# Modulation and gate steps emitted behind the linear attention, and ordered behind low parts of weights

## The chip, the cores and the metric

The kernel runs on one core of one Trainium2 chip. The metric is the device time of one execution in microseconds, the lower the better. Five engines work side by side, each through its own list of instructions, strictly in the order of that list: TensorE (PE, with its weight loads as PEld), VectorE (DVE), ScalarE (ACT), GpSimd (POOL) and SyncE (SP), which here only issues transfers.

## The reference

A trunk of two layers on 512 tokens of width 1024, in float32:

```python
for i in range(2):
    shift, scale, gate = split(silu(c) @ w_ada + b_ada, 3)
    h = rms_norm(x, ln_pre) * (1 + scale) + shift
    u = split_columns(h @ w_in)            # 3740 columns
    o_a = dilated_attention(...)           # group A
    o_b = nsa_attention(...)               # group B: compressed, selected, window
    o_c = rms_norm(gla_attention(...))     # group C: gated linear attention
    o_d = banded_attention(..., sinks)     # group D
    y = concat(o_j * silu(z_j)) @ w_out
    x = x + gate * rms_norm(y, ln_post)
```

`shift`, `scale` and `gate` of a layer come from the vector c alone: 1024 by 3072 weights a layer, used once.

## The kernel before

Products that need float32 accuracy are made of three: every weight block and every activation is split into a high part (`whi`, `HH`: a copy on ScalarE) and a low part (`wlo`, `HL`: a subtraction on VectorE, for weights in `split_w`, line 494), and high by high, high by low and low by high are added up on TensorE (`mm_T` line 541, `mm_TM` line 552). Weights of `w_in` come in pieces of 512 KB through four buffers `wraw`; their two parts have three buffers each.

A layer is one loop, `merge` (line 1274 on): the attention generators are run in the order C (linear attention), B, A, D, and between their steps the projections of `w_in` (`proj`) and the first part of the output product (`out1`) are emitted, in amounts by estimated costs. Emission sets priorities; the tile framework then sorts each engine's list by them and by readiness, and that list is fixed when the kernel is built. Attention steps are emitted with a lead in priority (the numbers HC, HB, HA, HD).

The steps that the change moves are those of `extras(l)` (line 375), a third generator, `bg` in `merge`. It holds what the coming layer's norm and this layer's residual need of `w_ada`:

- for layer 1, emitted during layer 0: 32 **modulation steps**, each a load `wmod` of 256 KB and one multiply and sum on VectorE (`mod`, line 306), with a tiny step on line 310 after every fourth;
- for each layer, two **gate columns** of eight **gate steps**: a load `wada` of 256 KB and one multiply and add on VectorE (`mac`, lines 364 and 366) into `aac`. After the eighth, `fin` loads two broadcast rows (`adab`, `adal`), sums `aac` over partitions on TensorE (`ada`, line 393), adds on VectorE (line 394) and multiplies on GpSimd (`gl`, line 396).

All these loads, `adab` and `adal` included, share one tile tag `ad` with **two buffers**, and `aac` has one. The loads are issued by SyncE, whose list also holds the loads of weights and those of the linear attention (`vs`, line 840).

How fast `extras` advances is set by the list TK of each layer, one number for C, B, A and D:

```python
def bg(cost):
    tick[0] += cost
    while tick[0] > pace:
        tick[0] -= pace
        next(BG[0], None)
for n_, (g, names, ratio, lead) in enumerate(steps):
    pace = LP[l]['TK'][min(n_, 3)]
```

`cost` is the estimated time of the projection step just emitted. `tick` is not reset between C, B, A and D.

Of the kernel before, what the change touches and what calls it, by code (L numbers as in the profile page):

```python
# [7 lines left out]
F32 = mybir.dt.float32  # L8
F32R = mybir.dt.float32r
AF = mybir.ActivationFunctionType  # L10
ALU = mybir.AluOpType
# [31 lines left out]
STP = 0  # L43

LP = [
    dict(HC=30, HB=[60, 200, 120], HA=60, HD=200, RC=0.9, RB=0.7, RA=1.4, RD=0.8, TK=[1.5, 1.5, 1.5, 1.5], CY=(1, 3, 3), PT=(4, 3),
         HO=(0, 2, 1, 3)),
    dict(HC=30, HB=[0, -60, 200], HA=100, HD=30, RC=0.9, RB=0.8, RA=0.8, RD=1.4, TK=[1.0, 6.0, 1.2, 0.7], CY=(0, 2, 2), PT=(1, 0),
         HO=(0, 3, 1, 2)),
]  # L50
WLO_MOD, WLO_POOL = 5, ()
# [183 lines left out]
def build(tc, A, out_d):  # L235
    nc = tc.nc
    PE, ACT, DVE, POOL, SP = nc.tensor, nc.scalar, nc.vector, nc.gpsimd, nc.sync
    with ExitStack() as ctx:
        def pool(name, bufs, **kw):
            return ctx.enter_context(tc.tile_pool(name=name, bufs=bufs, **kw))  # L240
# [8 lines left out]
        ad_p = pool('ad', B['ad'])  # L249
# [9 lines left out]
        def ps_t(tag, name):  # L259
            return ps.tile([128, 512], F32, tag=tag, name=name)  # L260
# [4 lines left out]
        def s_t(name, n, bufs=None):  # L265
            return sm_p.tile([128, n], F32, tag=name, name=name, **({'bufs': bufs} if bufs else {}))
# [16 lines left out]
        def load_mod(l, n, p, tag):  # L283

            wt = p.tile([128, 512], F32, tag=tag, name='wmod')
            SP.dma_start(out=wt, in_=A['w_mod'][l, n // 4, n // 2 % 2, n % 2])
            return wt
# [13 lines left out]
        def mod(l, n, wt, ss, gs):  # L301

            o, c = _P['bada'][0], n // 2
            h = n % 2
            init, dst = (tmp[:, c:c + 1], ss[:, c:c + 1]) if h else (pars[l][:, o + c:o + c + 1], tmp[:, c:c + 1])
            DVE.tensor_tensor_reduce(wt, wt, csr[:, 512 * h:512 * h + 512], 0.5, init, ALU.mult, ALU.add, dst)  # L306
            if n % 4 == 3:
                j = n // 4
                o = _P['lnpre'][0]
                DVE.scalar_tensor_tensor(gs[:, j:j + 1], ss[:, c:c + 1], 1.0, pars[l][:, o + j:o + j + 1], op0=ALU.add, op1=ALU.mult)  # L310
# [3 lines left out]
        def load_par(l):  # L314
            t = pp.tile([128, P_TOT], F32, tag='par', name='par')
            SP.dma_start(out=t, in_=A['par'][l])
            pars.append(t)

        WR = {}
        for ch in FIRST:  # L320
# [8 lines left out]
            elif ch in 'TQ':  # L329
                n = 'tm_c' if ch == 'T' else 't_cqk'  # L330
# [31 lines left out]
        def mac(acc, w, k, first):  # L362
            if first:
                DVE.tensor_scalar(acc, w, csil[:, k:k + 1], None, op0=ALU.mult)
            else:
                DVE.scalar_tensor_tensor(acc, w, csil[:, k:k + 1], acc, op0=ALU.mult, op1=ALU.add)

        def halves(t):
# [3 lines left out]
            DVE.tensor_tensor(out=lo, in0=t, in1=hi, op=ALU.subtract)  # L372
            return hi, lo

        def extras(l):

            units = []
            if l + 1 < DEPTH:
                load_par(l + 1)
                ss, gs = s_t('adass', 16, 2), s_t('adags', 8, 2)  # L380
                ada[l + 1] = (gs, ss)
                units = [(2, n) for n in range(32)]
            units += [(n, k) for n in range(2) for k in range(8)]
            gl[l] = []

            def fin(n, sb):
                acc = ps_t('s', 'ada')
                o = 512 * n
                br = ad_p.tile([128, 512], F32, tag='ad', name='adab')
                SP.dma_start(out=br, in_=A['rows'][l, 0, :, o:o + 512].to_broadcast([128, 512]))  # L390
                lr = ad_p.tile([128, 512], F32, tag='ad', name='adal')
                SP.dma_start(out=lr, in_=A['rows'][l, 1, :, o:o + 512].to_broadcast([128, 512]))
                PE.matmul(acc, ones.to_broadcast([128, 128]), sb, start=True, stop=True)
                DVE.tensor_tensor(out=br, in0=acc, in1=br, op=ALU.add)  # L394
                g = sz_p.tile([128, 512], F32, tag='sz', name='gl')
                POOL.tensor_tensor(out=g, in0=br, in1=lr, op=ALU.mult)
                gl[l].append(g)

            def load(n, k):
                if n == 2:  # L400
                    return load_mod(l + 1, k, ad_p, 'ad')
                wt = ad_p.tile([128, 512], F32, tag='ad', name='wada')
                SP.dma_start(out=wt, in_=A['w_gate'][l, n, k])
                return wt
            nxt = load(*units[0])
            prev = None
            for u, (n, k) in enumerate(units):
                yield
                wt = nxt
                if prev:  # L410
                    fin(*prev)
                    prev = None
                if n == 2:
                    mod(l + 1, k, wt, ss, gs)
                else:
                    if k == 0:
                        sb = ad_p.tile([128, 512], F32, tag='aac', name='aac', bufs=1)
                    mac(sb, wt, k, k == 0)
                    if k == 7:
                        prev = (n, sb)  # L420
                if u + 1 < len(units):
                    nxt = load(*units[u + 1])
            yield
            fin(*prev)
# [63 lines left out]
        def split_w(raw, n, eng=None):  # L488
            hi = w_p.tile([128, n], F32R, tag='whi', name='whi')
            lo = w_p.tile([128, n], F32R, tag='wlo', name='wlo')  # L490
            ACT.copy(hi, raw)  # L491
            nsplit[0] += 1
            eng = eng or (POOL if nsplit[0] % WLO_MOD in WLO_POOL else DVE)
            eng.tensor_tensor(out=lo, in0=raw, in1=hi, op=ALU.subtract)  # L494
            return hi, lo

        def load_piece(l, name, i, kk, ncol):
            if l == 0 and i == 0 and WR.get(name):
                raw = WR[name].pop()
            else:  # L500
                raw = raw_p.tile([128, kk * ncol], F32, tag='raw', name='wraw')
                o = W_OFF[name, i]
                SP.dma_start(out=raw, in_=A['w_in'][l, o:o + 128 * kk * ncol].rearrange('(p n) -> p n', p=128))
            hi, lo = split_w(raw, kk * ncol, DVE if l == 0 and name in ('tm_c', 't_cqk') else None)
            return [(hi[:, j * ncol:(j + 1) * ncol], lo[:, j * ncol:(j + 1) * ncol]) for j in range(kk)]
# [657 lines left out]
        def wo_piece(l, n):  # L1163
            k0, kk, c, nc_ = WO_PIECES[n]
            raw = raw_p.tile([128, kk * nc_], F32, tag='raw', name='wor')
            o = WO_OFF[n]
            SP.dma_start(out=raw, in_=A['w_out'][l, o:o + 128 * kk * nc_].rearrange('(p n) -> p n', p=128))
            if k0 == 6:
                res = []
                for j in range(kk):  # L1170
                    r = raw[:, nc_ * j:nc_ * (j + 1)]
                    hi, lo = qk_pair('wo2')
                    ACT.copy(hi, r)
                    DVE.tensor_tensor(out=lo, in0=r, in1=hi, op=ALU.subtract)
                    res.append((hi, lo))
                return res
            hi, lo = split_w(raw, kk * nc_)
            return [(hi[:, nc_ * j:nc_ * (j + 1)], lo[:, nc_ * j:nc_ * (j + 1)]) for j in range(kk)]
# [146 lines left out]
        for l in range(DEPTH):  # L1325
            for n in list(T):
                if l and n not in ('cvd', 'vc', 'dv', 'bg'):
                    del T[n]
            BG[0] = extras(l)
            pg = chain(proj(l, 1 if l else 2), out1(l))  # L1330
            PG[0] = pg
# [34 lines left out]
def make(arrays):  # L1366
    import concourse.bacc as bacc
    nc = bacc.Bacc("TRN2", target_bir_lowering=False, num_devices=1)
    A = {n: nc.dram_tensor('in_' + n, arrays[n].shape, F32, kind="ExternalInput").ap() for n in _INS}
    out = nc.dram_tensor('out_y', (S, D), F32, kind="ExternalOutput").ap()  # L1370
    with tile.TileContext(nc, schedule_with_timeline_sim=TLS) as tc:
        build(tc, A, out)
    return nc
# [8 lines left out]
```

## Time and profile before

| what | value |
|---|---|
| time, median of 3 runs | 697.35 us (696.06 to 697.5) |
| time of the profiled execution | 696.35 us |
| its span, first to last instruction | 694.6 us |
| mean granted clock of TensorE | 0.984 |
| busy: PE, DVE, ACT, POOL | 93%, 71%, 49%, 4% of the span |
| transfers | 87.89 MB, mean 127 GB/s |

The span is what the trace covers; 1.75 us of the profiled execution lie around it. Busy time of PE is modelled, so what counts in it is rather where it is idle. The stages in this trace: start-up with the first projections to 48 us, layer 0's linear attention to 152 us, its other attention to about 300 us, output product and the turn to layer 1 to 384 us, layer 1's linear attention to 494 us, its other attention to about 630 us, and the last output product.

### The profile page before, as it was taken

How to read it: one execution, taken by the hardware profiler on the slowest of the kernel's cores; microseconds unless marked ns; L12 is line 12 of the kernel's file. 1: busy time of each engine (PE TensorE's matmuls, PEld its weight loads, DVE VectorE, ACT ScalarE, POOL GpSimd, SP SyncE). 2: the span in 40 equal slices, each digit the busy share in tenths (PEclk: the TensorE clock that was granted, in tenths of full speed). 3: DMA queues.
4: the chain of work that ended last, by engine and by line, in shares of the span. 5: the costliest groups of instructions: out<-in, count | busy, mean ns of one | idle time of the engine just before them, and what ended most of it. 6: DMA issues, size and time to landing. Idle time of an engine off the chain costs nothing.

```text
span 694.6 us, 11875 instructions
## 1 busy us (share of the span) xinstructions
PE 649.3 (93%) x4460; PEld 525.3 (76%) x4460; DVE 492.8 (71%) x1255; ACT 340.3 (49%) x744; POOL 29.5 (4%) x57
## 2 busy tenths in 40 slices
PE   3899789999999999999998989899999999999996
PEld 1787666877777677779897768678877877778895
DVE  2984888667976878774698457742699858768656
ACT  7554344164664646654475253435655336435432
POOL 1000000000010000000111000000000000000000
PEclk9999999999999999999999979999999999999999
DMA  8945764568115342103543570222520021111142
GB/s 332 410 182 164 243 196 136 180 200 283 54 46 153 117 122 82 46 31 121 177 151 99 173 259 31 64 61 92 179 65 10 23 64 58 51 42 45 52 159 111
DMA packets 35283, 87.89 MB, mean 127 GB/s; under 512 B 3865, under 2 KB 7449, under 8 KB 35226
## 3 DMA queue, kind: packets, MB, share of 16 engines
q1 hardware_dynamic: 35226, 87.13, 38.0%
q8 instruction: 35, 0.57, 0.3%
q14 instruction: 22, 0.18, 0.1%
HBM read 81.88 MB, written 5.24 MB: 125 GB/s over the span
## 4 chain that ended last, share of the span: by engine, by line
PE 64%; DVE 14%; DMA 11%; ACT 5%; issue 3%; SPq 1%; POOL 1%; DVEq 0%; POOLq 0%; ACTq 0%
PE mmT L541 22%; PE yo L1185 9%; PE mmTM L552 6%; PE pT L787 5%; DMA wmod<-in_w_mod 4%; PE ob L801 3%; DMA vs<-vd 3%; DVE wlo L494 2%; PE sc L654 2%; PE a L735 2%; PE sc L655 2%; PE yo L1232 2%; PE od L1023 2%; PE oa L801 2%; DVE wmod L306 2%
## 5 line engine op out<-in xcount | busy, mean ns | idle before, releaser
L541 PE MATMUL mmT<-HH,whi 128*128 128x512 f32 (+1 forms) x352 | 143.0, 406 | 1.3 <-ACT x L622 1.3
L541 PE MATMUL mmT<-HL,whi 128*128 128x512 f32 (+1 forms) x352 | 142.2, 404 | 0.0
L541 PE MATMUL mmT<-HH,wlo 128*128 128x512 f32 (+1 forms) x352 | 142.0, 403 | 0.1
L773 ACT ACTIVATE p<-p,m 128x256 f32<-128x256 f32 (+3 forms) x128 | 68.7, 538 | 66.1 <-DVE m L771 60.7
L494 DVE TENSOR_TENSOR wlo<-wraw,whi 128x1024 fp32r<-128x1024 f32 (+3 forms) x60 | 72.2, 1205 | 38.5 <-ACT whi L491 38.3
L491 ACT CAST whi<-wraw 128x1024 fp32r<-128x1024 f32 (+3 forms) x60 | 61.5, 1027 | 67.2 <-PE mmT L541 46.0
L541 PEld LDWEIGHTS mmT<-HH,whi 128*128 128x128 f32 (+1 forms) x352 | 66.4, 189 | 15.7 <-issue 1.5
L541 PEld LDWEIGHTS mmT<-HH,wlo 128*128 128x128 f32 (+1 forms) x352 | 66.2, 188 | 14.9 <-DVE wlo L494 0.8
L541 PEld LDWEIGHTS mmT<-HL,whi 128*128 128x128 f32 (+1 forms) x352 | 66.6, 189 | 13.4 <-issue 0.5
L787 PE MATMUL pT<-cst,p 128*128 128x128 f32 x296 | 49.9, 280 | 3.5 <-DVE l L779 1.4
L552 PE MATMUL mmTM<-whi,HH 128*128 128x256 f32 (+1 forms) x160 | 48.4, 302 | 3.7 <-ACT HH L483 2.4
L787 PEld LDWEIGHTS pT<-cst,p 128*128 128x128 f32 x296 | 33.2, 140 | 21.2 <-issue 12.5
L771 DVE CUSTOM_DVE_ANT_0 p<-sc,cst 128x128 f32<-128x128 f32 (+3 forms) x96 | 44.9, 483 | 5.8 <-PE sc L655 5.4
L552 PE MATMUL mmTM<-whi,HL 128*128 128x256 f32 (+1 forms) x160 | 47.7, 299 | 0.3 <-DVE HL L484 0.3
L552 PE MATMUL mmTM<-wlo,HH 128*128 128x256 f32 (+1 forms) x160 | 47.5, 297 | 0.0
L1185 PE MATMUL yo<-wlo,HH 128*128 128x256 f32 x144 | 41.9, 291 | 0.0
L1185 PE MATMUL yo<-whi,HH 128*128 128x256 f32 x144 | 41.7, 290 | 0.0
L1185 PE MATMUL yo<-whi,HL 128*128 128x256 f32 x144 | 41.1, 286 | 0.0
L552 PEld LDWEIGHTS mmTM<-whi,HH 128*128 128x128 f32 x160 | 31.0, 194 | 6.1 <-ACT HH L483 3.5
L794 DVE COPY pt<-pT 128x256 f32<-128x256 f32 (+3 forms) x60 | 28.5, 499 | 8.5 <-PE pT L787 7.4
L654 PE MATMUL sc<-k,x 128*128 128x128 f32 (+3 forms) x96 | 32.2, 346 | 0.9 <-DVE adab L394 0.5
L552 PEld LDWEIGHTS mmTM<-whi,HL 128*128 128x128 f32 x160 | 30.9, 194 | 1.8 <-DVE HL L484 0.9
(271 smaller groups left out, 1326.1 us busy)
## 6 DMA issues: line engine op xcount, KB each, us to landing
wraw<-in_w_in SPq DMA_DIRECT2D x52, 512.0 KB
wmod<-in_w_mod SPq DMA_DIRECT2D x16, 512.0 KB
wmod<-in_w_mod SPq DMA_DIRECT2D x32, 256.0 KB
wada<-in_w_gate SPq DMA_DIRECT2D x32, 256.0 KB
wor<-in_w_out SPq DMA_DIRECT2D x12, 512.0 KB
w<-in_w SPq DMA_DIRECT2D x8, 512.0 KB
vs<-vd SPq DMA_DIRECT2D x24, 128.0 KB
x<-in_x SPq DMA_DIRECT2D x4, 512.0 KB
```

Of the source, the lines that this page charges most:

```text
L306: DVE.tensor_tensor_reduce(wt, wt, csr[:, 512 * h:512 * h + 512], 0.5, init, ALU.mult, ALU.add, dst)
L491: ACT.copy(hi, raw)
L494: eng.tensor_tensor(out=lo, in0=raw, in1=hi, op=ALU.subtract)
L541: PE.matmul(acc[:m], a, b, start=(n == 0), stop=(n == 23))
L552: PE.matmul(acc[:, :ncol], a, b, start=(n == 0), stop=(n == 23))
L654: PE.matmul(out, q[e][:, qs], k[e][0][:, ks], start=True, stop=False)
L771: DVE.tensor_tensor_reduce(p[:, c], sc[:, c], mask, -0.125, 1e38 if sink is None else sink[0][:, es[j]:es[j] + 1], ALU.add, ALU.min, m[:, ...
L773: ACT.activation(p[:, c], p[:, c], AF.Exp, bias=m[:, j:j + 1], scale=-1.0, accum_out=lsum[:, j:j + 1])
L787: PE.transpose(tp[:, b:b + 128], p[:, b:b + 128], C('ident'))
L794: DVE.tensor_copy(dst, src)
L801: PE.matmul(o[hs, q0:q1], vt[:, kb, vc:vc + 64], PT[:, 512 * kb:512 * kb + q1 - q0], start=(first and kb == 0), stop=(last and kb == 3), s ...
L1185: PE.matmul(acc[:, :n_], a, b, start=(n == 0), stop=(n == last))
```

## The change

In both layers TK is 99.0 for the linear attention and 1.6 for the rest. Before it was 1.5 throughout in layer 0, and 1.0, 6.0, 1.2, 0.7 in layer 1. `split_w` now notes the last `wlo` instruction in `LO`, and the modulation and gate steps are traced within `tc.issue_after(LO[0])`: an edge of order alone, without a semaphore, so that each stands in VectorE's list behind the low part that was emitted last. The arithmetic is the same. All line numbers behind `extras` are 4 higher in the changed kernel.

```diff
--- before.py
+++ after.py
@@ -43,9 +43,9 @@
 STP = 0
 
 LP = [
-    dict(HC=30, HB=[60, 200, 120], HA=60, HD=200, RC=0.9, RB=0.7, RA=1.4, RD=0.8, TK=[1.5, 1.5, 1.5, 1.5], CY=(1, 3, 3), PT=(4, 3),
+    dict(HC=30, HB=[60, 200, 120], HA=60, HD=200, RC=0.9, RB=0.7, RA=1.4, RD=0.8, TK=[99.0, 1.6, 1.6, 1.6], CY=(1, 3, 3), PT=(4, 3),
          HO=(0, 2, 1, 3)),
-    dict(HC=30, HB=[0, -60, 200], HA=100, HD=30, RC=0.9, RB=0.8, RA=0.8, RD=1.4, TK=[1.0, 6.0, 1.2, 0.7], CY=(0, 2, 2), PT=(1, 0),
+    dict(HC=30, HB=[0, -60, 200], HA=100, HD=30, RC=0.9, RB=0.8, RA=0.8, RD=1.4, TK=[99.0, 1.6, 1.6, 1.6], CY=(0, 2, 2), PT=(1, 0),
          HO=(0, 3, 1, 2)),
 ]
 WLO_MOD, WLO_POOL = 5, ()
@@ -372,6 +372,8 @@
             DVE.tensor_tensor(out=lo, in0=t, in1=hi, op=ALU.subtract)
             return hi, lo
 
+        LO = [None]
+
         def extras(l):
 
             units = []
@@ -410,14 +412,16 @@
                 if prev:
                     fin(*prev)
                     prev = None
-                if n == 2:
-                    mod(l + 1, k, wt, ss, gs)
-                else:
-                    if k == 0:
-                        sb = ad_p.tile([128, 512], F32, tag='aac', name='aac', bufs=1)
-                    mac(sb, wt, k, k == 0)
-                    if k == 7:
-                        prev = (n, sb)
+
+                with tc.issue_after(LO[0]):
+                    if n == 2:
+                        mod(l + 1, k, wt, ss, gs)
+                    else:
+                        if k == 0:
+                            sb = ad_p.tile([128, 512], F32, tag='aac', name='aac', bufs=1)
+                        mac(sb, wt, k, k == 0)
+                if n < 2 and k == 7:
+                    prev = (n, sb)
                 if u + 1 < len(units):
                     nxt = load(*units[u + 1])
             yield
@@ -491,7 +495,7 @@
             ACT.copy(hi, raw)
             nsplit[0] += 1
             eng = eng or (POOL if nsplit[0] % WLO_MOD in WLO_POOL else DVE)
-            eng.tensor_tensor(out=lo, in0=raw, in1=hi, op=ALU.subtract)
+            LO[0] = eng.tensor_tensor(out=lo, in0=raw, in1=hi, op=ALU.subtract).ins
             return hi, lo
 
         def load_piece(l, name, i, kk, ncol):
```

What the change makes of the lists, at three places.

**VectorE, layer 0, in attention B** (`p<-sc` with `m` and `p<-p,l,bg` are softmax steps, `wmod` and `aac` the moved steps). Before, at its second score tiles:

```order
L779 RECIPROCAL l<-l 128x2
L784 TENSOR_SCALAR p<-p,l,bg 128x256 x2
L646 TENSOR_TENSOR kl<-mmT,k_1886 64x512
L647 TENSOR_TENSOR kl<-mmT,k_1886 64x512
L794 COPY pt<-pT 128x2x128
L779 RECIPROCAL l<-l 128x1 x2
L771 ISA p,m<-sc,cst 128x512
```

Now, at the same softmax steps:

```order
L498 TENSOR_TENSOR wlo<-wraw,whi 128x1024
L306 ISA wmod,adass<-wmod,csr,tmp 128x512
L306 ISA adass 128x1
L306 ISA wmod,tmp<-wmod,csr,par 128x512
L306 ISA tmp 128x1
L306 ISA wmod,adass<-wmod,csr,tmp 128x512
L306 ISA adass 128x1
L310 SCALAR_TENSOR_TENSOR adags<-adass,par 128x1
L364 TENSOR_SCALAR aac<-wada,csil 128x512
L366 SCALAR_TENSOR_TENSOR aac<-wada,csil,aac 128x512 x7
L396 TENSOR_TENSOR adab<-ada,adab 128x512
L364 TENSOR_SCALAR aac<-wada,csil 128x512
```

All 32 modulation steps now stand between attention B's steps, and they end with this row of steps without a softmax step among them; the next one, `p<-sc` of 128x384, stands behind it. Before, all 32 stood among the linear attention's steps.

**TensorE, layer 1, at the start of attention B** (`kcp` makes the compressed keys, `scmp` their scores, `ada` sums a gate column). Before:

```order
L1096 MATMUL kcp<-hbuf,par 64x32 x4
L541 MATMUL mmT<-HL,whi 128x512
L1098 MATMUL kcp<-par,hbuf 128x64
L541 MATMUL mmT<-HH,wlo 128x512
L541 MATMUL mmT<-HH,whi 128x512
L541 MATMUL mmT<-HL,whi 128x512
L541 MATMUL mmT<-HH,wlo 128x512
L1113 MATMUL scmp_5133<-kc,x_4445 128x64
```

Now:

```order
L1100 MATMUL kcp<-hbuf,par 64x32 x4
L545 MATMUL mmT<-HH,whi 128x512
L545 MATMUL mmT<-HL,whi 128x512
L545 MATMUL mmT<-HH,wlo 128x512
L1102 MATMUL kcp<-par,hbuf 128x64
L395 MATMUL ada<-aac,ones 128x512 x2
L1117 MATMUL scmp_5133<-kc,x_4377 128x64
```

Both gate sums of layer 1 now stand ahead of the scores. In VectorE's list the 16 gate steps of layer 1 stand at the same place: the first behind the `wlo` that follows the step `hbuf` of line 1085 (now 1089), the last twelve without any other step among them than one `adab`. Before, they stood in layer 0's attention and around the turn to layer 1.

**SyncE, start of layer 1's linear attention** (`vd` and `vs` carry its values through memory and back). Before:

```order
L503 DMA wraw<-in_w_in 128x1024
L588 DMA vd<-v_tm_c 128x4x128 x2
L403 DMA wada<-in_w_gate 128x512 x2
L840 DMA vs<-vd 64x512
L833 DMA v_4182<-vd 64x4x128 x2
L840 DMA vs<-vd 64x512
L840 DMA vs<-vd 64x1x512 x10
L403 DMA wada<-in_w_gate 128x512 x2
L503 DMA wraw<-in_w_in 128x1024 x2
L403 DMA wada<-in_w_gate 128x512
```

Now:

```order
L507 DMA wraw<-in_w_in 128x1024
L592 DMA vd<-v_tm_c 128x4x128 x2
L507 DMA wraw<-in_w_in 128x1024
L844 DMA vs<-vd 64x512
L837 DMA v_4127<-vd 64x4x128 x2
L844 DMA vs<-vd 64x512
L844 DMA vs<-vd 64x1x512 x10
L507 DMA wraw<-in_w_in 128x1024 x9
```

The gate loads are gone from here, and one more piece of weights stands ahead of `vs`. They now stand behind the four pieces of weights that follow the loads `w` of attention B.

## Rows read from the trace of the kernel before

**Rows 1.** The page: span, and part 1, busy time of each engine in us (share of span), instructions.

```profile
span 694.6 us, 11875 instructions
...
PE 649.3 (93%) x4460; PEld 525.3 (76%) x4460; DVE 492.8 (71%) x1255; ACT 340.3 (49%) x744; POOL 29.5 (4%) x57
```

**Rows 2.** Busy time by stretch, us: stretch, length, then PE, PEld, DVE, ACT, POOL.

```profile
48.00:152.00 104.00, 94.86 (x809) 75.22 (x809) 76.57 (x177) 46.82 (x75) 2.97 (x6) 0.97 0.59 184
160.20:204.10 43.90, 42.76 (x253) 32.76 (x252) 37.25 (x119) 26.55 (x74) 1.30 (x1) 1.00 0.33 111
405.00:412.00 7.00, 3.64 (x16) 2.88 (x15) 5.49 (x9) 5.58 (x8) 0.00 (x0) 0.82 0.82 264
412.00:420.00 8.00, 8.00 (x27) 6.35 (x26) 3.30 (x9) 4.59 (x7) 0.00 (x0) 0.51 0.39 140
420.00:456.00 36.00, 33.46 (x450) 26.36 (x449) 27.96 (x59) 15.41 (x27) 4.66 (x5) 1.00 0.19 60
456.00:494.00 38.00, 37.41 (x312) 32.17 (x310) 12.21 (x17) 17.73 (x24) 0.27 (x2) 1.00 0.20 60
```

**Rows 3.** Groups by line, VectorE: busy us, mean ns, idle before them and its cause.

```profile
L366 DVE SCALAR_TENSOR_TENSOR aac<-wada,csil,aac 128x512 f32<-128x512 f32 x28 | 20.9, 747 | 12.2 <-DMA wada<-in_w_gate 12.0
...
L306 DVE CUSTOM_DVE_ANT_0 wmod<-wmod,csr,par 128x512 f32<-128x512 f32 x16 | 12.4, 775 | 8.0 <-DMA wmod<-in_w_mod 8.0
L306 DVE CUSTOM_DVE_ANT_0 wmod<-wmod,csr,tmp 128x512 f32<-128x512 f32 x16 | 12.0, 748 | 8.3 <-DMA wmod<-in_w_mod 8.1
...
L364 DVE TENSOR_SCALAR aac<-wada,csil 128x512 f32<-128x512 f32 x4 | 1.9, 480 | 0.8 <-DMA wada<-in_w_gate 0.8
```

**Rows 4.** The chain of waits, end of layer 0's linear attention: start, length, what.

```profile
125.07 3.68 DMA wmod<-in_w_mod
...
129.56 2.71 DMA wmod<-in_w_mod
...
133.08 2.75 DMA wmod<-in_w_mod
```

**Rows 5.** Timeline of SyncE, layer 1: start, length, issues.

```profile
371.72 0.33 SPq L392 DMA_DIRECT2D adal<-in_rows  x1
...
397.78 2.13 SPq L403 DMA_DIRECT2D wada<-in_w_gate  x2
400.41 0.81 SPq L503 DMA_DIRECT2D wraw<-in_w_in  x2
...
492.11 22.10 SPq L503 DMA_DIRECT2D wraw<-in_w_in  x8
```

**Rows 6.** Timeline of ScalarE, layer 1's linear attention.

```profile
404.94 1.05 ACT L491 CAST whi<-wraw 128x1024 fp32r<-128x1024 f32 x1 [6.37 <-DMA wraw<-in_w_in]
```

**Rows 7.** Timeline of TensorE: one gate product of layer 0, one wait of layer 1.

```profile
195.08 1.09 PE L393 MATMUL ada<-aac,ones 128*128 128x512 f32 x2
...
410.81 2.08 PE L857 MATMUL bp<-cst,la 128*128 128x128 f32 x8 [3.36 <-DVE la L853]
```

**Rows 8.** Timeline of VectorE: layer 0 and layer 1 behind the linear attention.

```profile
160.28 1.23 DVE L494 TENSOR_TENSOR wlo<-wraw,whi 128x1024 fp32r<-128x1024 f32 x1
...
379.34 0.75 DVE L366 SCALAR_TENSOR_TENSOR aac<-wada,csil,aac 128x512 f32<-128x512 f32 x1
...
496.87 1.22 DVE L494 TENSOR_TENSOR wlo<-wraw,whi 128x1024 fp32r<-128x1024 f32 x1
```

**Rows 9.** The chain of waits on TensorE, by runs of products.

```profile
188.63 2.92 PE ob L801 x14
...
208.66 0.91 PE pT L787 x6
...
460.74 2.88 PE mmTM L552 x24
...
494.80 4.32 PE mmT L541 x19
...
501.07 1.71 PE scmp L1113 x16
```

## What the change will do: the prediction

> **What bounds the kernel now.** I read the page first: TensorE is busy in 649.3 of 694.6 us [rows 1], so a change pays only where TensorE stands idle or runs at the lower clock. The table by stretch says where that is. In layer 0's linear attention TensorE is idle 9.1 of 104 us (104.00 less 94.86) at a granted clock of 0.97. At the start of layer 1's, from 405 to 412 us, it is idle 3.4 of 7 us, and the next 8 us run at 0.51, which is the lower level, 1.2 GHz [rows 2]. In the attention stages behind, it is nearly full, with VectorE as a close second: 37.25 of 43.9 us between 160.2 and 204.1 us. Third, the groups of VectorE: 28 gate steps at 747 ns, 4 at 480 ns, 32 modulation steps near 750 ns, with 16.1 us (8.0 and 8.1) in which VectorE waited for the modulation weights alone, and 12.8 us for gate weights [rows 3].
>
> Fourth, the chain of waits shows what such a wait is. With only two buffers, a load is issued when the step two before it is done. From the end of one modulation step to the start of the step after next, the chain holds a load of 2.71 to 3.68 us [rows 4]. Take 2.75 us: two steps take at least 2.75 + 0.75 = 3.5 us, however close they stand, against 1.5 us of work. This is the number that the forecast turns on.
>
> **Linear attention of layer 0: a gain of 6 us.** 32 steps by 0.75 us are 24 us that leave VectorE there, and 16.1 us of waiting with them. TensorE cannot gain more than its idle 9.1 us and about 3 us for the clock (3% of 104). Layer 1's linear attention is the same work nearly free of such steps, and from 420 to 456 us it still idles 2.5 of 36 us, or 7% [rows 2]; so the rest of the idle time, a little over 3 of 9 us, and most of the clock go: 6 us, bounds 2 and 12.
>
> **Linear attention of layer 1: a gain of 6 us.** SyncE issued two gate loads at 397.78, and two pieces of weights behind them at 400.41 [rows 5]. ScalarE waited 6.37 us for such a piece, until 404.94 [rows 6], with the steps behind it on which `bp` depends; TensorE waited 3.36 us for `bp` [rows 7], then came the 8 us at 0.51. In the new list a piece of weights stands ahead of the transfers `vs`, and no gate load stands in between, so this wait should go. Half of 8 us is 4 us for the clock; with the idle 3.4 us that is 7.4 at most. I take 6, bounds 2 and 8.5 (the other 18% of clock between 405 and 412 added).
>
> **Attention B of layer 0: a loss of 26 us.** TK of 99 stops `extras`, but `tick` is kept, so at the first step of B the arrears are emitted at once. By VectorE's list, from the `wlo` at 160.28 [rows 8] to the eighth gate step there now stand:
> - the steps that filled 37.25 us between 160.2 and 204.1 us [rows 2], less three gate steps (2.2), one `adab` (0.7) and one first gate step (0.5), plus three later `wlo` (3.7): 37.5 us;
> - 32 modulation steps (24 us), their eight small ones (1.2) and eight gate steps (0.5 + 7 x 0.75 = 5.7): 31 us.
>
> That is 68.5 us, to 228.8. The last 14 of these 40 loaded steps stand with almost nothing between them (two `wlo` and some softmax scaling, 4.4 us): they take seven pairs of 3.5 us, 24.5 us, where work is 10.5 + 4.4. So 9.6 us of waiting come on top: 238.4. Then `adab` waits for its row, 2.75 us like any load, and takes 0.7: softmax goes on at 241.8.
>
> TensorE meets `ada` in its list much earlier. Before, it met its first one at 195.08 [rows 7]; now 25 more `mmT` stand ahead of it (0.228 us each by 19 in 4.32) and 72 more `mmTM` (0.12 by 24 in 2.88) [rows 9], 14.3 us, with one group of output products (2.92), 20 transposes (0.15 by 6 in 0.91) and three pairs of scores (about 0.9): 21.1 us, to 216.2. From there its next scores need VectorE. 241.8 - 216.2 is 25.6, say 26 us idle. Bounds: 17 if no load is waited for (softmax on at 232.3 with `adab`), 33 if VectorE also keeps the 6.65 us that it idled in that stretch before.
>
> **Attention B of layer 1: a loss of 32 us.** This is the sharpest term. Both `ada` stand ahead of `scmp` in TensorE's list, so no score of B starts before the sixteenth gate step. The first stands behind the `wlo` that ended at 496.87 + 1.22 = 498.1 [rows 8], which itself waits for pieces issued at 492.11 [rows 5]. Two steps find their weights loaded: 499.6. Steps 3 to 8 are three pairs: 510.1. `adab`'s row, its add and step 9 follow: 2.75 + 0.7 + 0.5, to 514. From the issue of `adal` (371.72) to the next gate step behind it (379.34) the trace has 7.6 us, since `gl` must first free the buffer for that step's load [rows 5, 8]: step 10 at 521.6, done at 522.4. Steps 11 to 16 are three more round trips: 532.9, and `ada` 0.6: `scmp` at 533.5 instead of 501.07 [rows 9]. TensorE has the same `mmT` ahead of that point as before, so 32 us are idle. Bounds: 10 if the steps cost only their 13 us of work on VectorE; 40 if every one of six round trips takes the longer load of 3.68 and SyncE's weights, which stand between, add some.
>
> **The clock after that: a loss of 5 us.** The row at 412 us shows half clock for 8 us after a wait of 3.4 us [rows 2, 7]: about 4 us lost each time. Two long waits, the first broken up: 5, bounds 0 and 8. Edits at nothing: `LO` itself is no instruction, and the moved loads are the same bytes; `gl` is needed only at the output products, some 60 and 130 us later.
>
> **Sum**, against the profiled execution's own 696.35 us (1 us below the median of the three runs): 696.35 - 6 - 6 + 26 + 32 + 5 = 747.35, so **747 us**. With all bounds one way: 696.35 - 12 - 8.5 + 17 + 10 = 703, and 696.35 - 2 - 2 + 33 + 40 + 8 = 773.
>
> **The rivals.**
>
> *The two buffers hide the loads.* The runs then cost VectorE's own work alone: 17 and 10 us, and with 12 us gained and 3 of clock lost the time is 714. The Trainium skill ("Trainium Kernel Development and Optimization", section Best Practices) asks for double buffering so that transfers overlap with compute. By that rule this is what two buffers are for. The trace speaks against it: VectorE waited 16.1 us for modulation weights with these buffers [rows 3], since the step on one buffer lasts 0.75 us and the load of the other 2.75. Chance 0.10.
>
> *Faster: the runs fall into idle time of VectorE.* From 456 to 494 us it works only 12.2 of 38 us [rows 2]; if all 16 gate steps of layer 1 were done by the time TensorE comes to `ada`, and layer 0's were spread likewise, only the gains would be left: 696.35 - 12 = 684. It decides whether the sixteenth step ends before about 500.5. Against it: the order is fixed, the first stands behind a `wlo` at 496.87, and 16 steps take 8 us even without any load. Chance 0.06.
>
> *No change.* If gains and losses were both small because TensorE's backlog covers each move, 697. The lists rule out that nothing moves. Chance 0.03.
>
> *Worse.* The gate loads queue behind 512 KB pieces on SyncE, and the long waits leave TensorE at 1.2 GHz for more than 8 us each time: 773 and above. Chance 0.09.
>
> **How the numbers follow.** The forecast keeps 0.72, since both losses rest on lists and on one measured round trip. Within its case the time may lie between 727 and 768. The range takes the double-buffering case in and leaves out the fast cases and the worst: 712 to 770. Faster by over 0.2% (1.4 us, about what a measurement tells from no change here) 0.06, within it 0.03, slower 0.91.
>
> **What would show it.** In the new trace: no modulation step before about 155 us, and 32 of them behind, the last and the gate steps in pairs 3.5 us apart; `ada` on TensorE idle before it by 10 us or more in layer 0, and again by some 30 us in layer 1 with `aac` as releaser; ScalarE's 6.37 us wait gone and `bp` without a wait. I am wrong if TensorE is busy while the sixteen gate steps run, or if these take under 20 us.

## The result: 58.6 us slower, and the profile after

| | before | changed |
|---|---|---|
| time, median | 696.7 us (4 runs, 692.58 to 697.5) | 755.33 us (4 runs, 754.66 to 757.84) |
| ratio | | 1.0861, 95% interval 1.081 to 1.0912 |
| profiled execution, its span | 696.35, 694.6 us | 757.84, 756.1 us |
| mean granted clock | 0.984 | 0.941 |

The median before is that of the three runs shown above and a fourth of 692.58 us. The forecast was 747 us with 712 to 770 as its range; the change of the median is 58.6 us where 50 were forecast. The page of the changed kernel, against [rows 1]:

```profile
span 756.1 us, 11883 instructions
...
PE 654.9 (87%) x4460; PEld 528.2 (70%) x4460; DVE 491.6 (65%) x1255; ACT 340.4 (45%) x744; POOL 29.3 (4%) x57
```

The engines run as many working instructions as before: PE is busy 5.6 us longer, DVE 1.2 us less, but the span grew by 61.5 us. So 55.9 us of it are idle time of TensorE. To say where, I cut the profiled execution of each kernel at the start of four rows of TensorE's timeline: the first `hid` of layer 0 (the first products of attention B's key compression, at the end of the linear attention), the last `tp` of the turn (the transposes of the norm's output), the last row of `hid` in layer 1, the last `mmT`. Lengths of the stages in us, here and for the experiments below:

| kernel | layer 0, linear | layer 0, rest and turn | layer 1, linear | layer 1, attention | last `mmT` at |
|---|---|---|---|---|---|
| before | 151.9 | 219.0 | 119.6 | 137.3 | 627.9 |
| changed | 142.6 | 252.0 | 116.0 | 178.8 | 689.4 |
| e1_layer0 | 142.7 | 252.1 | 134.4 | 137.6 | 666.9 |
| e2_layer1 | 151.6 | 225.5 | 116.1 | 176.7 | 669.9 |
| e3_edge | 152.0 | 225.6 | 134.9 | 137.7 | 650.2 |
| e4_reset | 142.2 | 231.0 | 116.3 | 151.8 | 641.3 |
| e5_no_edge | 150.6 | 216.7 | 115.6 | 164.5 | 647.3 |
| e6_four_bufs | 142.7 | 240.9 | 116.2 | 161.9 | 661.7 |
| e7_control | 142.6 | 252.1 | 115.9 | 177.1 | 687.8 |
| e8_late | 155.8 | 218.0 | 118.5 | 137.5 | 629.8 |
| e9_best_order | 148.7 | 217.1 | 120.2 | 138.1 | 624.1 |
| e10_before_four | 151.2 | 217.6 | 113.8 | 137.4 | 620.0 |
| e11_best_four | 151.7 | 216.3 | 117.4 | 138.6 | 624.0 |

The change gains 9.3 and 3.6 us in the two linear attentions and loses 33.0 and 41.5 us behind them: 61.6, and nothing after the last `mmT`. Single profiled executions of one kernel differ by some us (e8_late has the kernel before's list of TensorE in layer 0's linear attention and takes 3.9 us longer there; e7_control has all lists of the changed kernel), so differences under 4 us in this table are read only where several kernels share them, as in the third column (115.6 to 116.3 in six of them).

The table by stretch of the changed kernel (columns as in [rows 2]) has the lost stretches:

```profile
48.00:142.50 94.50, 90.90 (x811) 73.25 (x809) 52.46 (x103) 46.47 (x75) 3.21 (x6) 1.00 0.35 111
160.00:186.00 26.00, 22.00 (x128) 17.75 (x128) 22.55 (x76) 11.11 (x32) 0.00 (x0) 0.87 0.49 145
213.80:235.60 21.80, 0.00 (x1) 0.00 (x0) 9.49 (x18) 0.85 (x1) 0.00 (x0) 0.57 0.56 177
235.60:246.00 10.40, 8.82 (x22) 5.69 (x23) 6.48 (x15) 3.41 (x8) 2.50 (x3) 0.50 0.19 53
...
440.00:476.80 36.80, 33.00 (x435) 24.84 (x434) 24.52 (x53) 14.72 (x26) 2.94 (x4) 0.95 0.18 58
522.00:558.00 36.00, 2.71 (x3) 1.00 (x4) 12.01 (x18) 1.29 (x4) 1.26 (x1) 0.53 0.48 155
558.00:566.00 8.00, 8.00 (x29) 6.58 (x27) 4.13 (x8) 0.00 (x0) 1.34 (x2) 0.50 0.12 34
566.00:580.00 14.00, 13.46 (x72) 10.20 (x72) 12.16 (x44) 7.76 (x20) 0.00 (x0) 0.92 0.12 39
```

TensorE does nothing from 213.8 to 235.6 and 2.7 us of work in the 36 us from 522. In the first row it idles 3.6 of 94.5 us at full clock, where it idled 9.1 of 104 at 0.97 [rows 2]. TensorE's timeline says who it waited for:

```profile
171.78 0.63 PE L1148 MATMUL pcT<-cst,pc 128*128 128x128 f32 x4 [3.44 <-DVE pc L1143]
...
235.64 2.08 PE L395 MATMUL ada<-aac,ones 128*128 128x512 f32 x2 [21.84 <-DVE aac L366]
...
239.69 0.80 PE L658 MATMUL sc<-k,x 128*128 128x512 f32 x1 [1.34 <-DVE adab L396]
...
431.36 1.16 PE L861 MATMUL bp<-cst,la 128*128 128x128 f32 x8 [0.82 <-DVE la L857]
...
533.29 2.04 PE L395 MATMUL ada<-aac,ones 128*128 128x512 f32 x2 [11.29 <-DVE aac L366]
...
557.34 2.05 PE L395 MATMUL ada<-aac,ones 128*128 128x512 f32 x2 [22.01 <-DVE aac L366]
```

Three waits at `ada`, 21.84 in layer 0 and 11.29 + 22.01 in layer 1, all for `aac`, the sum of a gate column. `bp`, which had waited 3.36 us [rows 7], waits 0.82. VectorE's timeline shows what a row of steps is, first in layer 0 (where a modulation step ahead of `pc` waits, and where the row of gate steps stands), then in layer 1:

```profile
168.14 0.75 DVE L306 CUSTOM_DVE_ANT_0 wmod<-wmod,csr,par 128x512 f32<-128x512 f32 x1 [1.57 <-DMA wmod<-in_w_mod]
...
224.46 1.54 DVE L366 SCALAR_TENSOR_TENSOR aac<-wada,csil,aac 128x512 f32<-128x512 f32 x2 [2.35 <-DMA wada<-in_w_gate]
227.94 1.64 DVE L366 SCALAR_TENSOR_TENSOR aac<-wada,csil,aac 128x512 f32<-128x512 f32 x2 [1.94 <-DMA wada<-in_w_gate]
...
536.91 0.69 DVE L396 TENSOR_TENSOR adab<-ada,adab 128x512 f32<-128x512 f32 x1 [3.77 <-DMA adab<-in_rows]
537.52 0.48 DVE L364 TENSOR_SCALAR aac<-wada,csil 128x512 f32<-128x512 f32 x1
545.79 1.54 DVE L366 SCALAR_TENSOR_TENSOR aac<-wada,csil,aac 128x512 f32<-128x512 f32 x2 [7.79 <-DMA wada<-in_w_gate]
549.29 1.58 DVE L366 SCALAR_TENSOR_TENSOR aac<-wada,csil,aac 128x512 f32<-128x512 f32 x2 [1.97 <-DMA wada<-in_w_gate]
552.86 1.54 DVE L366 SCALAR_TENSOR_TENSOR aac<-wada,csil,aac 128x512 f32<-128x512 f32 x2 [2.00 <-DMA wada<-in_w_gate]
556.44 0.75 DVE L366 SCALAR_TENSOR_TENSOR aac<-wada,csil,aac 128x512 f32<-128x512 f32 x1 [2.04 <-DMA wada<-in_w_gate]
```

In layer 1 the last loaded steps come in pairs that start at 545.79, 549.29, 552.86 and 556.44 (there only the first of a pair is left), 3.5 us apart, with 1.5 us of work and 2 us of waiting for `wada` in each; ahead of them is one wait of 7.79 us. SyncE and GpSimd have the reason for that one:

```profile
538.02 0.33 SPq L394 DMA_DIRECT2D adal<-in_rows  x1
543.12 10.85 SPq L405 DMA_DIRECT2D wada<-in_w_gate  x7
...
541.83 1.26 POOL L398 TENSOR_TENSOR gl<-adab,adal 128x512 f32<-128x512 f32 x1 [34.56 <-DMA adal<-in_rows]
```

`adal` takes one of the two buffers and gives it back only after GpSimd's `gl`, which ends at 543.09; the next gate load is issued at 543.12, 5.1 us after `adal`. In VectorE's groups the waiting for modulation weights fell from 16.1 us [rows 3] to 5.9, and that for gate weights rose from 12.0 to 29.0 (in the 28 steps of line 366):

```profile
L366 DVE SCALAR_TENSOR_TENSOR aac<-wada,csil,aac 128x512 f32<-128x512 f32 x28 | 21.0, 749 | 29.3 <-DMA wada<-in_w_gate 29.0
...
L306 DVE CUSTOM_DVE_ANT_0 wmod<-wmod,csr,par 128x512 f32<-128x512 f32 x16 | 12.0, 748 | 1.7 <-DMA wmod<-in_w_mod 1.6
L306 DVE CUSTOM_DVE_ANT_0 wmod<-wmod,csr,tmp 128x512 f32<-128x512 f32 x16 | 12.0, 748 | 4.3 <-DMA wmod<-in_w_mod 4.3
```

### The profile page after: what moved, and what is told of

It reads as the page before. It is cut to its first block, busy times and chain, and to the rows that moved or that the text cites. A ratio compares the mean times of both kernels' runs of the same rounds, so it can differ in the third digit from the quotient of the medians.

```text
span 756.1 us, 11883 instructions
## 1 busy us (share of the span) xinstructions
PE 654.9 (87%) x4460; PEld 528.2 (70%) x4460; DVE 491.6 (65%) x1255; ACT 340.4 (45%) x744; POOL 29.3 (4%) x57
## 3 DMA queue, kind: packets, MB, share of 16 engines
q1 hardware_dynamic: 35226, 87.13, 34.8%
## 4 chain that ended last, share of the span: by engine, by line
PE 59%; DMA 16%; DVE 12%; ACT 7%; issue 3%; SPq 1%; POOL 1%; DVEq 0%; POOLq 0%; ACTq 0%
PE mmT L545 20%; PE yo L1189 8%; PE mmTM L556 6%; DMA wada<-in_w_gate 5%; PE pT L791 4%; DMA vs<-vd 3%; PE ob L805 2%; DMA wmod<-in_w_mod 2%; PE sc L658 2%; PE a L739 2%; PE sc L659 2%; DMA wraw<-in_w_in 2%; PE yo L1236 2%; PE od L1027 2%; ACT whi L495 2%
## 5 line engine op out<-in xcount | busy, mean ns | idle before, releaser
L495 ACT CAST whi<-wraw 128x1024 fp32r<-128x1024 f32 (+3 forms) x60 | 61.6, 1028 | 79.5 <-PE mmT L545 68.5
L545 PEld LDWEIGHTS mmT<-HH,wlo 128*128 128x128 f32 (+1 forms) x352 | 66.5, 189 | 14.5 <-issue 0.5
L395 PE MATMUL ada<-aac,ones 128*128 128x512 f32 x8 | 7.3, 1010 | 55.2 <-DVE aac L366 55.1
L791 PEld LDWEIGHTS pT<-cst,p 128*128 128x128 f32 x296 | 34.3, 143 | 18.4 <-issue 10.3
L395 PEld LDWEIGHTS ada<-aac,ones 128*128 128x128 f32 x8 | 1.8, 280 | 57.7 <-issue 35.0
L1189 PE MATMUL yo<-whi,HH 128*128 128x256 f32 x144 | 41.7, 290 | 0.0
L366 DVE SCALAR_TENSOR_TENSOR aac<-wada,csil,aac 128x512 f32<-128x512 f32 x28 | 21.0, 749 | 29.3 <-DMA wada<-in_w_gate 29.0
L658 PE MATMUL sc<-k,x 128*128 128x128 f32 (+3 forms) x96 | 35.1, 375 | 2.6 <-DVE adab L396 2.5
```

The costliest lines, as they stand in the source:

```text
L545: PE.matmul(acc[:m], a, b, start=(n == 0), stop=(n == 23))
L658: PE.matmul(out, q[e][:, qs], k[e][0][:, ks], start=True, stop=False)
L791: PE.transpose(tp[:, b:b + 128], p[:, b:b + 128], C('ident'))
L1189: PE.matmul(acc[:, :n_], a, b, start=(n == 0), stop=(n == last))
```

## The experiments

Two edits make the change: the numbers TK, with `tick` carried over, and the edge of order behind `wlo`. All times below are medians with the ratio to the kernel before on the same chip (696.3 us for the first four, 696.65 for the next four, 695.17 for the last three).

### Each layer alone, and the edge alone

In e1_layer0 and e2_layer1 one TK list goes back to its old numbers, in e3_edge both:

```diff
 # e1_layer0: layer 1
-TK=[99.0, 1.6, 1.6, 1.6]
+TK=[1.0, 6.0, 1.2, 0.7]
 # e2_layer1: layer 0
-TK=[99.0, 1.6, 1.6, 1.6]
+TK=[1.5, 1.5, 1.5, 1.5]
 # e3_edge: both of these
```

> The changed kernel with layer 1's TK put back to [1.0, 6.0, 1.2, 0.7]; layer 0's and the edge stay. My theory (each layer's burst of steps holds TensorE by itself, and the two simply add): layer 0's part alone, the gain of 9.4 us in its linear attention and the loss of 33 us in its attention B, so 697 - 9 + 33 = 721, between 716 and 726, with ada in layer 0 waiting about 22 us again. Rival (the edge is what costs, wherever the steps are): most of the 58 us stays, 740 or more. Rival (layer 0's burst is made up for later, because TensorE's backlog covers it): below 705.

> The changed kernel with layer 0's TK put back to 1.5 throughout; layer 1's and the edge stay. My theory: layer 1's part alone, a gain of 3 to 6 us in its linear attention and a loss of 37 us for the 16 steps ahead of scmp with 4 us of clock behind: 697 - 4 + 37 + 4 = 734, between 728 and 741, and ada in layer 1 waiting about 33 us in two pieces. Rival (the edge): 740 or more. Rival (layer 1's steps were late because layer 0's were): below 715.

> The changed kernel with both TK lists of before: only the edge of order is left of the change. My theory: an edge without a semaphore costs what the few steps it moves cost, 692 to 704. Rival (steps ordered behind wlo are what holds the loads back and makes them stand in rows): 720 or more.

Measured: e1_layer0 735.03 us (1.0557, 1.0516 to 1.0598), e2_layer1 737.98 (1.0598, 1.0553 to 1.0643), e3_edge 717.47 (1.031, 1.0272 to 1.0348). Only the second came out in its range, and that in part by luck: of its 41.7 us, 6.5 lie in layer 0 behind the linear attention (225.5 against 219.0), where the expectation had nothing. Its two waits at `ada` are as expected, 11.39 + 21.24 us. The edge alone, with the old TK, costs 21 us, 2.5 us short of the rival's range. By the stage table 15.3 of them lie in layer 1's linear attention and 6.6 in layer 0 behind its own, and e1_layer0 has the same 15 us there, which is why it came out at 735 and not 721. Counted from e3_edge the layers do add: 717.47 + 17.56 + 20.51 = 755.54, against 755.33 for the change.

How the edge costs 15 us is seen in e3_edge, in VectorE's timeline and below it TensorE's:

```profile
406.15 1.57 DVE L366 SCALAR_TENSOR_TENSOR aac<-wada,csil,aac 128x512 f32<-128x512 f32 x2 [7.47 <-DMA wada<-in_w_gate]
...
412.47 0.69 DVE L609 COPY ca<-mmT 16x512 f32<-16x512 f32 x1
```

```profile
413.31 0.77 PE L545 MATMUL mmT<-HH,whi 128*128 128x512 f32 x1 [5.83 <-DVE ca L609]
...
436.85 0.90 PE L904 MATMUL kp<-cst,kd 128*128 128x128 f32 x3 [2.69 <-DVE kd L900]
440.88 1.12 PE L952 MATMUL att<-kq 32*64 32x64 f32 x30 [3.13 <-DVE kq L946]
```

In the kernel before, the scheduler was free to put layer 1's first gate column early into layer 0's attention (235.80 to 258.47 us), the second around the turn. The edge ties each step to the `wlo` emitted last, so in e3_edge both columns stand at the start of layer 1's linear attention, from 395.88 to 441.97. There a gate step waits 7.47 us for its load, `ca`, the first link of the linear attention, stands behind it on VectorE and comes at 412.47; TensorE waits 5.83 us for it, then 2.69 for `kd` and 3.13 for `kq`, two of VectorE's results in the linear attention, among whose steps the second column stands. That is 11.7 of the 15.3 us; the clock there is 0.91 (0.94 before). The edge adds no instruction and no wait of its own; what it takes away is the freedom to start early.

### The arrears, and the change without the edge

```diff
 # e4_reset, in merge
                 pace = LP[l]['TK'][min(n_, 3)]
+                tick[0] = 0.0
 # e5_no_edge, in extras
-                with tc.issue_after(LO[0]):
+                if True:
```

> The changed kernel with tick set to 0 at the start of each attention step, so that no arrears are emitted at once; TK, and with it the empty linear attention, and the edge stay. 27 us of modulation steps still lie in layer 0's attention B, A and D. My theory (the row of steps costs, not the work): layer 1's 41 us go nearly all, layer 0's ada wait of 22 us too; 755 - 41 - 22 = 692, and some us for VectorE's added work in layer 0's attention: 690 to 708. Rival (VectorE has no room for 27 us more in layer 0's attention, in rows or not): 712 to 722. Rival (the flush is not the cause): 745 or more.

> The changed kernel without the edge of order; both TK lists as changed. In layer 1 only the second gate column now stands as a row ahead of smc, the first stands in layer 0's time. My theory (rows of steps cost by their length): half of layer 1's loss stays, about 18 to 20 us, and its linear attention keeps its gain of 3.5; in layer 0 the modulation steps float back into the end of the linear attention and the row of gate steps is broken up, so layer 0 costs 0 to 5: about 715, between 706 and 724. Rival (the edge makes the whole loss with these TK too): 700 or less. Rival (TK makes it all): 745 or more.

Measured: e4_reset 709.1 us (1.0186, 1.0149 to 1.0223), e5_no_edge 712.82 (1.0228, 1.0192 to 1.0264). Without the carry-over of `tick`, or without the edge, most of the loss is gone, 46.2 or 42.5 us of 58.6. The four corners of the two edits are about 696.5 (neither edit), 717.5 (edge), 712.8 (TK) and 755.3 (both): the two cost 21.2 and 16.2 us alone against their own runs of the kernel before, and 21.2 more together. TK empties the linear attention and lets all arrears be emitted at one point; the edge forbids the scheduler to spread them from there. Only both make the rows in both layers at full length.

In e5_no_edge the first column of layer 1 is again in layer 0's time (243.81 to 263.54 us), and of two `ada` only the second waits, 21.17 us; the stage costs 27.2 us, where 16 steps cost 41.5:

```profile
491.73 1.12 PE L395 MATMUL ada<-aac,ones 128*128 128x512 f32 x2
...
515.40 2.08 PE L395 MATMUL ada<-aac,ones 128*128 128x512 f32 x2 [21.17 <-DVE aac L366]
```

So a row does not cost by its number of steps, as my theory had it: half of the steps cost two thirds, for the wait behind `adal` (7.47 us here) stands in this column whole. That the time is inside its range is partly luck: layer 1 lost 27 us in place of 18 to 20, and layer 0 gained 3.6 us where 0 to 5 of loss were expected.

e4_reset came out 1 us above its range and 3 us below the rival's, and does not decide between them. No `ada` waits over 3.3 us there, yet layer 0's rest is 12.0 us longer than before, and layer 1's attention is still 14.5 us longer than before. Before, none of the 16 gate steps lay in that stage. The stretches of layer 1 show no long hole, only small idle times and two stretches at a lower clock:

```profile
489.50:525.00 35.50, 34.07 (x212) 27.59 (x212) 28.19 (x78) 17.12 (x35) 0.00 (x0) 0.90 0.51 164
525.00:565.00 40.00, 34.47 (x208) 26.84 (x207) 29.33 (x77) 13.84 (x36) 1.29 (x1) 0.99 0.39 130
565.00:600.00 35.00, 34.34 (x176) 25.55 (x176) 31.18 (x102) 18.41 (x49) 3.71 (x5) 0.92 0.07 18
```

The clock accounts for 3.6 + 2.8 us of it (35.5 x 0.10 and 35 x 0.08). So steps that are spread out are not free in an attention stage either, but in layer 1 they cost a third of what the row costs.

### The round trip: four buffers

```diff
-B = dict(raw=4, w=3, mx=3, v4=5, dv=2, ad=2, ...)
+B = dict(raw=4, w=3, mx=3, v4=4, dv=2, ad=4, ...)
 # e7_control: v4=4 alone
```

> The changed kernel with four buffers for the steps' loads in place of two (v4 gets four in place of five, to make room). Layer 1's row of 16 steps keeps its place. My theory (a row's time is the round trip of its loads over its buffers): four loads overlap, so the 38.7 us from layer 1's first gate step to its last fall to 22 to 28, and layer 0's wait at ada from 22 to under 8, its clock loss with it: 755 - 13 - 17 = 725, between 716 and 736. Rival (the loads themselves or the one queue that issues them are the limit, so that more buffers help nothing): 748 or more.

> The changed kernel with v4 at four buffers and nothing else: the control for the run with four buffers. VectorE's list is the changed kernel's own, so every theory expects 753 to 758.

Measured: e6_four_bufs 729.21 us (1.0463, 1.0422 to 1.0504), e7_control 756.61 (1.0844, 1.0812 to 1.0877). The control is the changed kernel again, so 27.4 us go with two more buffers. VectorE and TensorE of e6_four_bufs in layer 1:

```profile
507.19 0.48 DVE L364 TENSOR_SCALAR aac<-wada,csil 128x512 f32<-128x512 f32 x1
...
516.39 0.75 DVE L366 SCALAR_TENSOR_TENSOR aac<-wada,csil,aac 128x512 f32<-128x512 f32 x1 [1.41 <-DMA wada<-in_w_gate]
...
525.42 3.11 DVE L366 SCALAR_TENSOR_TENSOR aac<-wada,csil,aac 128x512 f32<-128x512 f32 x4 [1.20 <-DMA wada<-in_w_gate]
529.07 0.75 DVE L366 SCALAR_TENSOR_TENSOR aac<-wada,csil,aac 128x512 f32<-128x512 f32 x1 [0.53 <-DMA wada<-in_w_gate]
```

```profile
517.28 2.04 PE L395 MATMUL ada<-aac,ones 128*128 128x512 f32 x2 [7.06 <-DVE aac L366]
529.96 2.04 PE L395 MATMUL ada<-aac,ones 128*128 128x512 f32 x2 [10.64 <-DVE aac L366]
```

From the first gate step to the end of the last it takes 22.6 us (507.19 to 529.82) where the changed kernel takes 38.7 (518.49 to 557.19), with the same steps in nearly the same order, and TensorE waits 7.06 + 10.64 in place of 11.29 + 22.01. Work of the 16 steps is 11.5 us (2 x 0.48 + 14 x 0.75), so of 38.7 us at least 16.1 were the round trip on two buffers. The stage is still 24.6 us longer than before: hiding loads does not help what stands in a row ahead of `smc` on VectorE (the masked scores of the compressed keys).

In layer 0 no `ada` waits any more, as expected, but the stage fell by only 11.1 us (252.0 to 240.9), where my sum had about 17. There the idle time has moved ahead: between 160 and 190 us TensorE idles 10.3 us while VectorE is nearly full:

```profile
160.00:190.00 30.00, 19.66 (x100) 14.17 (x99) 26.84 (x93) 10.85 (x28) 0.00 (x0) 0.89 0.67 195
```

VectorE's waits for gate weights fell from 29.0 to 5.2 us and those for modulation weights from 5.9 to 1.7, 28.0 us together, which fits the 27.4 gained, though with four buffers the scheduler also sorted the lists anew (264 of VectorE's 1255 places differ). The other 31 us of the loss remain with loads that are mostly hidden. The Trainium skill ("Trainium Kernel Development and Optimization", section Best Practices) asks for double buffering so that transfers overlap with compute; here two buffers left 29.0 us of waiting for gate weights, since a step lasts 0.75 us and a load in the chain 2.71 to 3.68 [rows 4].

### Towards a version that beats both

```diff
 # e8_late, on the kernel before (two buffers, no edge)
-TK=[1.0, 6.0, 1.2, 0.7]   (layer 1)
+TK=[1.0, 1.0, 1.0, 1.0]
-            tick = [0.0]
+            tick = [-24.0 if l else 0.0]
 # e9_best_order: the same with -36.0, and in layer 0
-TK=[1.5, 1.5, 1.5, 1.5]
+TK=[99.0, 1.6, 1.6, 1.6]
 # e10_before_four, on the kernel before: v4=4, ad=4
 # e11_best_four: e9_best_order and v4=4, ad=4
```

> The kernel before (no edge) with layer 1's TK at 1.0 throughout and tick starting at -24 in layer 1: the second gate column then stands in the second half of layer 1's linear attention, where VectorE is idle for more than half of the time, and its loads behind the transfers vs; the first stands in layer 0 as before. My theory: the gain of 3.5 us in layer 1's linear attention comes without any loss, 692 to 695. Rival (steps among the linear attention's delay TensorE there, wherever in it): 697 or more.

> The kernel before (no edge) with layer 0's TK as the change has it, layer 1's at 1.0 throughout and tick starting at -36 there: layer 1's second gate column stands between the linear attention's last steps and attention B, where VectorE works 11 of 33 us. My theory (TK alone gains 3.7 us in layer 0 and 3.9 in layer 1's linear attention, as the run without the edge shows by stage, and only the row of eight steps ahead of smc loses): 697 - 3.7 - 3.9 = 689, between 686 and 693. Rival (eight steps cost TensorE time wherever they stand in layer 1): 694 or more.

> The kernel before with four buffers for the steps' loads (v4 at four in place of five), nothing else. My theory (what the modulation steps cost layer 0's linear attention is the wait for their loads on two buffers): 5 to 9 us of the 9.4 come back, 688 to 692. Rival (their work on VectorE costs it): 695 to 698.

> The same as e9_best_order with four buffers. My theory: the loads are hidden in both layers, 684 to 690, at least 1 us below e9_best_order. Rival (with the steps spread out, two buffers are enough): within 1 us of e9_best_order.

Measured: e8_late 697.32 us (1.0004, 0.998 to 1.0027), e9_best_order 694.08 (0.9989, 0.9967 to 1.0011), e10_before_four 691.3 (0.9946, 0.992 to 0.9971), e11_best_four 693.3 (0.9973, 0.9949 to 0.9997). Only e10_before_four beats the kernel before clearly, by 0.5%; e11_best_four does by less, and e8_late and e9_best_order can't be told from it. So three expectations failed, and each time the rival's time came: eight gate steps in the late linear attention, where VectorE works a third of the time, are not free, and with the steps spread out two buffers do nearly as well as four (0.8 us between e9_best_order and e11_best_four, whose waiting for gate weights is 16.5 and 5.8 us). e9_best_order shows one way in which the steps cost:

```profile
464.58 0.75 DVE L366 SCALAR_TENSOR_TENSOR aac<-wada,csil,aac 128x512 f32<-128x512 f32 x1 [7.17 <-DMA wada<-in_w_gate]
...
477.67 0.69 DVE L372 TENSOR_TENSOR lo<-sq,hi 128x512 fp32r<-128x512 f32 x1
```

```profile
478.41 0.50 PE L988 MATMUL ms<-lo,hblk 128*128 128x512 f32 x1 [1.31 <-DVE lo L372]
```

The second gate step holds VectorE for 7.17 us (`adal` and `gl` again), the later ones push `lo` back, and TensorE waits 1.31 us for it. With the executions' own spread, the rest of the 4.6 us by which this stage is longer than in e5_no_edge stays unexplained.

e10_before_four lies in its expected range, but by luck: it is faster for another reason than I gave. Its modulation steps wait 7.1 us in place of 16.1, but layer 0's linear attention gains under 1 us by the stage table; 5.8 us come from layer 1's:

```profile
L306 DVE CUSTOM_DVE_ANT_0 wmod<-wmod,csr,tmp 128x512 f32<-128x512 f32 x16 | 11.9, 746 | 6.4 <-DMA wmod<-in_w_mod 6.4
L306 DVE CUSTOM_DVE_ANT_0 wmod<-wmod,csr,par 128x512 f32<-128x512 f32 x16 | 11.7, 748 | 0.7 <-DMA wmod<-in_w_mod 0.7
...
381.41 1.54 DVE L366 SCALAR_TENSOR_TENSOR aac<-wada,csil,aac 128x512 f32<-128x512 f32 x2
...
382.82 0.48 SPq L840 DMA_DIRECT2D vs<-vd  x1
...
407.48 1.16 PE L857 MATMUL bp<-cst,la 128*128 128x128 f32 x8 [0.21 <-DVE la L853]
```

The last gate step of the kernel before:

```profile
408.25 0.75 DVE L366 SCALAR_TENSOR_TENSOR aac<-wada,csil,aac 128x512 f32<-128x512 f32 x1
```

With four buffers the lists are sorted anew, and the second gate column of layer 1 ends at 382.95, just as SyncE issues the first of the transfers `vs` (382.82), and its loads are all in front of them; in the kernel before its last step stood at 408.25. `bp` then waits 0.21 us in place of 3.36 [rows 7]. The profiled execution is the fastest of twelve, 2.8 us under their median, so the 5.8 us are rather too much; and v4 at four buffers was tried alone only on the changed kernel (e7_control), not here.

## Why the prediction was right, and where it was off

Term by term, against the stage table and the rows above:

- **Linear attention of layer 0**: forecast -6, measured -9.3, inside its bounds of 2 and 12. Of 9.1 us idle 5.5 went, and busy time fell by 4.0 (94.86 to 90.90) at full clock; I had let only a little over 3 us of idle time go. The first modulation step stands at 150.93 and not behind 155, since the stage ahead of it ended 9.3 us earlier.
- **Linear attention of layer 1**: forecast -6, measured -3.6, inside its bounds. The mechanism is shown: where ScalarE waited 6.37 us for a piece of weights [rows 6], its longest such wait ahead of `bp` is now 1.06, `bp` waits 0.82, and from 432 to 440 us the clock is 1.00:

```profile
426.81 1.05 ACT L495 CAST whi<-wraw 128x1024 fp32r<-128x1024 f32 x1 [1.06 <-DMA wraw<-in_w_in]
```

  What I missed is that some of it is given back further on: from 440 to 476.8 TensorE idles 3.8 us at 0.95, where the stretch from 420 to 456 had 2.5 us at 1.00 [rows 2]. Over the whole stage busy time fell by 2.6 us, through the clock, and idle time by only 1.0.
- **Attention B of layer 0**: forecast 26 us idle, measured 21.84 + 1.34 at the place named, 23.2. The 3.44 us before it, where modulation steps and a wait of 1.57 us for their weights held `pc` (the rows at 168.14 and 171.78), were not in the forecast; with them it is 26.6. The last gate steps of the row are pairs 3.5 us apart, as forecast. That the size fits is partly luck: counted from the same `wlo` (160.28 before, 149.79 now) VectorE needed 85.8 us to the eighth gate step, where 78.1 were forecast, and TensorE 64.0 us to `ada`, where 55.9 were; both were 8 us late, and the difference stayed.
- **Attention B of layer 1**: forecast 32 us idle, measured 11.29 + 22.01 = 33.3. Steps 11 to 16 are three round trips, and the wait for the tenth was taken from the trace as 7.6 us and measured 7.79. The row itself was sized too short, 34.8 us (498.1 to 532.9) against 38.7: steps 3 to 8 took 13.4 us in place of 10.5, and `adab`'s row 3.77 in place of 2.75. So `scmp` came 37.0 us later than before, counted from the `wlo` ahead of the row, where 32.4 were forecast; only 33.3 of it are idle, and the two `ada`, 4.1 us, take the rest.
- **The clock after that**: forecast +5 with bounds 0 and 8. This is the term that was mis-sized. The stage losses beyond the idle time are 33.0 - 26.6 = 6.4 and 41.5 - 33.3 = 8.2, 14.6 us together. The rows at lower clock give nearly as much, 14.5: 160 to 186 us (26 x 0.13 = 3.4), 235.6 to 246 (5.2), 246 to 262 at 0.95 (0.8), 558 to 566 (4.0), 566 to 580 (1.1). By layer they fit less well, 9.4 against 6.4 in layer 0 and 5.1 against 8.2 in layer 1, so the near match is luck. In layer 1 the difference is about the two `ada` themselves, 4.1 us at half clock, which stood ahead of this stage before; in layer 0 it stays open. By TensorE's busy time, which grew by 3.4 and 8.6 us in the two stages, it is 12.0. Each of these is more than twice the 5 us, and over the bound of 8. I had counted two waits and 4 us for each, less something; there were three waits with such a stretch behind them, the short one in layer 0 included.
- **`LO` at nothing**: the sum needed no price for it, since the lists that I read were made with it. But the text gave the rows to the arrears of `tick` alone (the steps that TK held back and `merge` then emits at once), and that is half of the cause: without the edge 42.5 us of the loss are gone.

The sum closes: -9.3 - 3.6 + 26.6 + 33.3 + 14.6 = 61.6 on 696.35 is 757.9, and the profiled execution has 757.84. It closes by construction, as the 14.6 is what the stages leave beyond the waits. The other terms' misses (-3.3, +2.4, +0.6 and +1.3) nearly cancel; of the 10.5 us between the forecast sum and the profiled execution 9.6 are in the last term. Against the median of 755.33 the forecast is 8 us short.

Of the rivals, the first (two buffers hide the loads, 714) falls by the 29.0 us of waiting and by the 27.4 us that two more buffers give back. "Faster" and "no change" fall with the rows of steps, and "worse" (773 and above) was not reached, though its mechanism is there in part: TensorE was at half clock for 10 us or so behind the long waits. Not tried, and so open, is whether TensorE would have found work if `ada` stood later in its list; VectorE's row, ahead of `smc` there as well, speaks against it.

## What to carry to other kernels

Before moving loaded steps out of one stage, count them in the list of the stage they go to: a row of them on a double buffer takes one load per buffer turn (here 3.5 us per pair against 1.5 us of work), and whatever is behind them in the same in-order list waits for the whole row. Look for the counter that lets deferred work be emitted at one point, and for an order edge that forbids spreading it; alone (the changed TK, the edge) they cost 16 and 21 us here, together 58.6. If a stage waits for loads, try more buffers before moving the work: that was the one version that clearly gained, by 0.5%, though not because the waits that I had in view were hidden, but because a column of loads came in front of other transfers.

## What the hardware showed that was not expected

In this trace the time at the lower clock grows far less than the wait before it. Two more rows of the table by stretch, behind the waits of 3.44 us and of 22.01 us:

```profile
172.00:180.00 8.00, 7.65 (x35) 5.42 (x34) 6.79 (x25) 3.70 (x12) 0.00 (x0) 0.57 0.47 134
557.00:568.00 11.00, 10.66 (x35) 8.89 (x36) 6.07 (x18) 1.50 (x5) 1.34 (x2) 0.50 0.09 28
```

After 3.44 us of waiting TensorE ran 8 us at 0.57, after 21.84 us 10.4 us at 0.50 (the row from 235.6), after 11.29 and 22.01 us, with one `ada` between, 11 us at 0.50. By these rows a wait costs 3.4 to 5.5 us (8 x 0.43, 11 x 0.50) on top of its own length, and a short one more than half as much as a long one. It is no fixed price: in e3_edge TensorE ran from 413.3 to 418 us at 0.50 behind the wait of 5.83 us, 2.4 us lost (4.7 x 0.50), less than behind the shorter 3.44. And no single long wait is needed: in e4_reset the clock between 489.5 and 525 us is 0.90, with 1.4 us idle in all.
